# Seven block products for eight: from the MLPs' first half, 256 columns moving, to their second half, 512 columns moving

## The chip, the cores and the metric

The kernel runs on one core of one Trainium2 chip. The metric is the device time of one execution in microseconds; the kernel before takes 1494.91 us, the median of three runs (1493.44 to 1496.66).

## What is computed

A decoder trunk of two layers on 512 tokens with 1024 features. Each layer has a token mixer (a Mamba-2 SSD in layer 0, an HGRN2 in layer 1), a norm, a squared-ReLU MLP with 4096 hidden features, a second norm, and a gated embedding. The change touches the MLPs:

```python
def sq_relu_mlp(h, w1, w2):
    a = jax.nn.relu(h @ w1)
    return (a * a) @ w2

h = layer_norm(DEEPNORM_ALPHA * x + mix, ln_g[i, 0], ln_b[i, 0])
h = layer_norm(DEEPNORM_ALPHA * h + sq_relu_mlp(h, mlp_w1[i], mlp_w2[i]), ln_g[i, 1], ln_b[i, 1])
x = h + jax.nn.sigmoid(h @ ple_w_gate[i]) * (p[i] @ ple_w_proj[i])
```

## The kernel before

Every large product is made of three matmuls on fp32r operands (`mm3`, L109 to L112): each operand is split into a high part (a cast on ScalarE, ACT) and a low part (a subtraction on VectorE, DVE), and high x high, high x low and low x high are summed in PSUM. Weights come in units of 128 x 1024 floats, 512 KB: `unit` (L98) loads one through SP's queue and splits it; the split parts live in two pools, `whi` and `wlo`, of five slots each, so a sixth unit is split only when TensorE (PE) is through with the first. Splits stand some 100 places early in the program (`LEAD`). The operand named first after the arrow in a profile row is the one that moves, the second is the stationary one.

`mlp_and_gate` (L345) has two halves, cut into eight parts e of four hidden tiles each:

- `hidden(e)` makes hidden features, 128 at a time, transposed: the weights are stationary, and the 512 tokens of h.T move. A plain tile is 8 x 3 matmuls with 512 columns moving (`project`, L127). The first four tiles (e = 0) are made by halves of the tokens, 256 columns at a time, while the last tokens' norm is still under way. The result goes through ReLU and square on ACT and is split.
- `out_project(e)` multiplies the four tiles with four row tiles of `w2`: tokens are stationary, 512 columns of weights move. For each of four token chunks and two column halves it takes 12 matmuls, and DVE adds the bank to `acc` (L223): 96 matmuls and eight adds for each e.

Of the 16 pairs of hidden tiles, the first three are plain. The other 13 use Winograd's form of Strassen's product (`strassen`, L309): seven products of blocks instead of eight, with half of the tokens as a block. So each matmul moves 256 columns, and a pair costs 7 x 4 x 3 = 84 of them instead of 48 with 512. Its sums cost DVE work: sums of h.T's blocks once per layer (`block_sums`, from an unsplit copy of h.T that the norm's `keep` makes), four 512-wide sums of weights for each pair and 3.5 units to split instead of two (`weight_sums`), and seven 256-wide sums of the products out of PSUM (L329 to L343), with one copy on ACT.

The order of the work is set by the table `ORDER`: h0 b0 h1 o0 h2 o1 ... h7 o6 o7, with o7 done token chunk by token chunk, each followed by the second norm and its transposes. Engines run their instructions in the order of the program, as a scheduler with the leads has laid it out; pools decide when a tile can be written again. Four PSUM banks `pj` serve the products, two `py` the mixers and the gate. SBUF is full: the pool `b8` has nine slots of 8 KB a partition, four of which hold h.T in its two parts. GpSimd (POOL) does nothing but a few memsets at the start.

Of the kernel before, what the change touches and what calls it, by code (L numbers as in the profile page):

```python
# [9 lines left out]
F32R = mybir.dt.float32r  # L10
# [32 lines left out]
def trunk(ctx: ExitStack, tc, a):  # L43
# [24 lines left out]
    def f32(t):  # L68
        return t.bitcast(F32)

    two = dict(xs=2, sz=2, cv=2, cm=2, cbm=2)
    bufs = dict(ssd=dict(two, ss=2), mlp0=dict(z=2, S=3), hgrn=dict(two, xs=4, sz=4, cv=4, y=2, pv=2, btok=2), mlp1=dict(z=2, S=3))
# [24 lines left out]
    # ---------------------------------------------------------------- weights  # L97
    def unit(src, lead=LEAD):  # L98
        n = src.shape[1]
        with tc.high_priority(offset=lead):  # L100
            raw = mk(raws, [P, 1024], "raw")
            nc.sync.dma_start(raw[:, :n], src)
            hi = mk(whip, [P, 1024], "whi", F32R)
            nc.scalar.copy(hi[:, :n], raw[:, :n])  # L104
            lo = mk(wlop, [P, 1024], "wlo", F32R)
            nc.vector.tensor_sub(lo[:, :n], raw[:, :n], f32(hi[:, :n]))  # L106
        return hi, lo

    def mm3(out, sh, sl, mh, ml, start, stop):  # L109
        nc.tensor.matmul(out, sh, mh, start=start, stop=False)  # L110
        nc.tensor.matmul(out, sh, ml, start=False, stop=False)  # L111
        nc.tensor.matmul(out, sl, mh, start=False, stop=stop)  # L112

    class Split:
        """[128, n, 512] as high and low parts, in slots of four rows each."""
# [11 lines left out]
    def project(src, xs, ps, m=P, tok=slice(0, T)):  # L127
        """ps[m, tok] = W[:, tile].T @ x.T for a weight unit of eight row tiles."""
# [5 lines left out]
    # ---------------------------------------------------------------- constants  # L134
# [35 lines left out]
    # ---------------------------------------------------------------- layer norm and friends  # L170
# [7 lines left out]
    def layer_norm(c, gb):  # L178
        """acc[:, c] = LN(acc[:, c])"""
# [13 lines left out]
    def transpose_split(src, dst, c, keep=None):  # L193
        """dst[:, k, chunk c] = src[tokens, k-th 128 features].T, split; unsplit in keep"""
        sl = slice(c * P, (c + 1) * P)
        for q in range(2):
# [8 lines left out]
            if keep is not None:  # L205
                nc.scalar.copy(keep[q][:, :, sl], v)
# [18 lines left out]
    def out_project(w, xs, first, after=None, scale=None):  # L225
        """w: the four units of four row tiles, by halves of the columns; after(c): what follows the last of chunk c"""
# [12 lines left out]
    def norm(i):  # L239
        """the norm's result, transposed and split, and what makes its chunk c"""  # L240
        gb = ln_params(i)
        h_s = Split(8)
        keep = [mk(b8, [P, 4, T], "b8") for _ in range(2)] if i % 2 == 0 else None

        def chunk(c):
            layer_norm(c, gb)
            transpose_split(acc[:, c, :], h_s, c, keep)

        return h_s, chunk, keep
# [3 lines left out]
    def block_sums(h_s, ht):  # L253
        """the four plain and four summed blocks of h.T, as (high, low) of a row tile k"""
        b = [[ht[k][:, :, 256 * t : 256 * t + 256] for k in range(2)] for t in range(2)]

        def plain(t, k):
            sl = slice(256 * t, 256 * t + 256)
            return lambda i: (h_s.h(4 * k + i, sl), h_s.l(4 * k + i, sl))

        def summed(f, t):
            nc.scalar.copy(t[:, 0], f)
            nc.vector.tensor_sub(t[:, 1], f, f32(t[:, 0]))
            return lambda i: (t[:, 0, i, :], t[:, 1, i, :])

        sums, prev = [], None
        for i in range(4):
            f = mk(w4, [P, 4, 256], "ab"[i % 2])
            if i == 0:
                nc.vector.tensor_add(f, b[1][0], b[1][1])  # L270
            elif i == 1:
                nc.vector.tensor_sub(f, prev, b[0][0])
                s2 = f
            elif i == 2:
                nc.vector.tensor_sub(f, b[0][0], b[1][0])
            else:
                nc.vector.tensor_sub(f, b[0][1], s2)
            prev = f
            t = tmp("S", [P, 2, 4, 256], F32R) if i < 3 else mk(b8, [P, 2, 4, 256], "b8", F32R)
            sums.append(summed(f, t))  # L280
        return [plain(0, 0), plain(0, 1), plain(1, 1)] + sums

    def weight_sums(src1, src2):
        """the seven blocks of two weight units: B11, B21, B22, T1, T2, T3, B21 - T2, as (high, low, column)"""
        h = 512
        with tc.high_priority(offset=LEAD):
            r1, r2 = mk(raws, [P, 1024], "raw"), mk(raws, [P, 1024], "raw")
            nc.sync.dma_start(r1, src1)
            nc.sync.dma_start(r2, src2)

            def split(f, n=1024):
                hi = mk(whip, [P, 1024], "whi", F32R)
                nc.scalar.copy(hi[:, :n], f)  # L293
                lo = mk(wlop, [P, 1024], "wlo", F32R)
                nc.vector.tensor_sub(lo[:, :n], f, f32(hi[:, :n]))  # L295
                return hi, lo

            w1 = split(r1)
            t1, t3 = mk(w4, [P, 1024], "a"), mk(w4, [P, 1024], "b")
            nc.vector.tensor_sub(t1[:, :h], r2[:, :h], r1[:, :h])  # L300
            nc.vector.tensor_sub(t1[:, h:], r2[:, h:], t1[:, :h])
            w2 = split(t1)
            nc.vector.tensor_sub(t3[:, :h], r2[:, h:], r2[:, :h])
            nc.vector.tensor_sub(t3[:, h:], r1[:, h:], t1[:, h:])
            w3 = split(t3)
            w4_ = split(r2[:, h:], h)
        return (*w1, 0), (*w1, h), (*w4_, 0), (*w2, 0), (*w2, h), (*w3, 0), (*w3, h)

    def strassen(blocks, src1, src2, z):  # L309
        """z[:, m] = W[:, tile m].T @ h.T for two weight units"""  # L310
        a11, a12, a22, s1, s2, s3, s4 = blocks
        b11, b21, b22, t1, t2, t3, t4 = weight_sums(src1, src2)

        def product(ps, x, w):
            hi, lo, c0 = w
            for k in range(4):
                c = slice(c0 + k * P, c0 + k * P + P)
                mm3(ps, hi[:, c], lo[:, c], *x(k), k == 0, k == 3)

        def pair():  # L320
            return bank(psj, "pj")[:, :256], bank(psj, "pj")[:, :256]

        z11, z12, z21, z22 = z[:, 0, :256], z[:, 1, :256], z[:, 0, 256:], z[:, 1, 256:]
        x1, u2, u3, u5 = (tmp(tag, [P, 256]) for tag in ("x1", "u2", "u3", "u5"))
        p1, p6 = pair()
        product(p1, a11, b11)
        nc.scalar.copy(x1, p1)
        product(p6, s2, t2)
        nc.vector.tensor_add(u2, p6, x1)  # L329
        p7, p5 = pair()  # L330
        product(p7, s3, t3)
        nc.vector.tensor_add(u3, p7, u2)
        product(p5, s1, t1)
        nc.vector.tensor_add(u5, p5, u2)
        nc.vector.tensor_add(z22, p7, u5)
        p2, p3 = pair()
        product(p2, a12, b21)
        nc.vector.tensor_add(z11, p2, x1)
        product(p3, s4, b22)
        nc.vector.tensor_add(z12, p3, u5)  # L340
        p4 = bank(psj, "pj")[:, :256]
        product(p4, a22, t4)
        nc.vector.tensor_add(z21, p4, u3)  # L343

    def mlp_and_gate(layer, h_s, ht, last):  # L345
        """acc holds the normed h. Returns the next x, transposed and split, with x in acc."""
        w1, w2 = a[f"w1_{layer}"], a[f"w2_{layer}"]

        def hidden(e):
            s = Split(4)  # L350
# [693 lines left out]
```

## Time and profile before

| | before |
|---|---|
| median of three runs | 1494.91 us |
| span of the profiled execution | 1492.3 us |
| PE busy | 1479.3 us, 8848 matmuls |
| weight loads on PE (PEld) | 1280.9 us |
| DVE busy | 1096.4 us |
| ACT busy | 711.2 us |
| POOL busy | 0.9 us |
| HBM traffic | 150.07 MB, 101 GB/s mean |

The span runs from the first to the last instruction of one profiled execution; the timed runs hold 2.6 us more. Busy times of matmuls are modelled and overlap their neighbours, so what a stream of matmuls costs is read from start to start. PEld overlaps PE. A group's line gives the source line, engine, operation, tiles and shapes, the count, then busy us and mean ns, then the idle time before the group and what ended it.

### The profile page before, as it was taken

How to read it: one execution, taken by the hardware profiler on the slowest of the kernel's cores; microseconds unless marked ns; L12 is line 12 of the kernel's file. 1: busy time of each engine (PE TensorE's matmuls, PEld its weight loads, DVE VectorE, ACT ScalarE, POOL GpSimd, SP SyncE). 2: the span in 40 equal slices, each digit the busy share in tenths (PEclk: the TensorE clock that was granted, in tenths of full speed). 3: DMA queues.
4: the chain of work that ended last, by engine and by line, in shares of the span. 5: the costliest groups of instructions: out<-in, count | busy, mean ns of one | idle time of the engine just before them, and what ended most of it. 6: DMA issues, size and time to landing. Idle time of an engine off the chain costs nothing.

```text
span 1492.3 us, 21964 instructions
## 1 busy us (share of the span) xinstructions
PE 1479.3 (99%) x8848; PEld 1280.9 (86%) x8848; DVE 1096.4 (73%) x1786; ACT 711.2 (48%) x968; POOL 0.9 (0%) x8
## 2 busy tenths in 40 slices
PE   8999999999999999999999999999999999999998
PEld 5888888888989999888778998989898999998887
DVE  6998677797886777776844767769787777777673
ACT  5777455563564434444334453543364444444342
POOL 0000000000000000000000000000000000000000
PEclk9999999999999999999999999999999999999999
DMA  6433223332233323244223222222123333324322
GB/s 237 169 102 111 98 100 113 100 113 85 71 99 99 113 82 103 88 139 129 94 71 114 86 66 77 70 72 72 57 72 99 114 113 100 110 79 150 115 71 71
DMA packets 41621, 150.07 MB, mean 101 GB/s; under 512 B 4624, under 2 KB 5136, under 8 KB 41392
## 3 DMA queue, kind: packets, MB, share of 16 engines
q1 hardware_dynamic: 41520, 148.67, 30.1%
q8 instruction: 70, 1.15, 0.3%
q14 instruction: 31, 0.25, 0.1%
HBM read 146.49 MB, written 2.16 MB: 100 GB/s over the span
## 4 chain that ended last, share of the span: by engine, by line
PE 97%; DMA 1%; DVE 1%; ACT 1%; issue 0%; SPq 0%; ACTq 0%; DVEq 0%
PE pj L110 29%; PE pj L111 28%; PE pj L112 28%; PE py L782 1%; PE py L591 1%; PE pt L200 1%; PE pm L561 1%; PE py L596 1%; PE py L792 1%; PE py L827 1%; DMA raw<-in_wg 1%; DVE wlo L106 0%; PE pt L549 0%; PE py L880 0%; PE py L112 0%; PE py L110 0%
## 5 line engine op out<-in xcount | busy, mean ns | idle before, releaser
L110 PE MATMUL pj<-whi,b 128*128 128x512 f32 (+1 forms) x1096 | 401.5, 367 | 0.5 <-ACT z L414 0.5
L111 PE MATMUL pj<-wlo,b 128*128 128x512 f32 (+1 forms) x1096 | 399.3, 364 | 0.5 <-DVE wlo L106 0.5
L112 PE MATMUL pj<-whi,b 128*128 128x512 f32 (+1 forms) x1096 | 399.8, 365 | 0.0
L110 PE MATMUL pj<-b,whi 128*128 128x256 f32 (+1 forms) x1024 | 348.0, 340 | 2.1 <-ACT whi L104 2.1
L112 PE MATMUL pj<-b,wlo 128*128 128x256 f32 (+1 forms) x1024 | 344.2, 336 | 0.0
L111 PE MATMUL pj<-b,whi 128*128 128x256 f32 (+1 forms) x1024 | 343.7, 336 | 0.0
L104 ACT CAST whi<-raw 128x1024 fp32r<-128x1024 f32 x192 | 201.4, 1050 | 229.6 <-PE pj L111 133.4
L106 DVE TENSOR_TENSOR wlo<-raw,whi 128x1024 fp32r<-128x1024 f32 x192 | 233.9, 1220 | 64.4 <-ACT whi L104 62.4
L111 PEld LDWEIGHTS pj<-wlo,b 128*128 128x128 f32 x1096 | 206.8, 189 | 32.2 <-DVE wlo L106 1.0
L110 PEld LDWEIGHTS pj<-whi,b 128*128 128x128 f32 x1096 | 206.6, 189 | 32.3 <-ACT z L414 0.7
L112 PEld LDWEIGHTS pj<-whi,b 128*128 128x128 f32 x1096 | 206.7, 189 | 31.7 <-issue 0.2
L110 PEld LDWEIGHTS pj<-b,whi 128*128 128x128 f32 x1024 | 194.5, 190 | 22.0 <-ACT whi L104 4.7
L112 PEld LDWEIGHTS pj<-b,wlo 128*128 128x128 f32 x1024 | 194.4, 190 | 20.3 <-DVE b L150 1.7
L111 PEld LDWEIGHTS pj<-b,whi 128*128 128x128 f32 x1024 | 194.6, 190 | 18.3 <-issue 1.9
L293 ACT CAST whi<-raw 128x1024 fp32r<-128x1024 f32 (+1 forms) x52 | 43.4, 835 | 136.2 <-PE pj L112 110.4
L223 DVE TENSOR_TENSOR acc<-pj,acc 128x512 f32<-128x512 f32 x120 | 81.6, 686 | 35.0 <-PE pj L112 34.5
L110 PE MATMUL pj<-S,whi 128*128 128x256 f32 x312 | 87.4, 280 | 0.0
L111 PE MATMUL pj<-S,whi 128*128 128x256 f32 x312 | 87.0, 279 | 0.0
L112 PE MATMUL pj<-S,wlo 128*128 128x256 f32 x312 | 87.0, 279 | 0.0
L295 DVE TENSOR_TENSOR wlo<-raw,whi 128x1024 fp32r<-128x1024 f32 (+1 forms) x52 | 49.7, 957 | 35.0 <-ACT whi L293 35.0
L293 ACT CAST whi<-a 128x1024 fp32r<-128x1024 f32 x26 | 27.3, 1050 | 94.8 <-PE pj L111 45.5
L110 PEld LDWEIGHTS pj<-S,whi 128*128 128x128 f32 x312 | 58.7, 188 | 0.0
(217 smaller groups left out, 1810.6 us busy)
## 6 DMA issues: line engine op xcount, KB each, us to landing
raw<-in_w SPq DMA_DIRECT2D x128, 512.0 KB, 3.4
raw<-in_wssd SPq DMA_DIRECT2D x40, 512.0 KB, 3.4
a<-csd SPq DMA_DIRECT2D x16, 512.0 KB, 4.0
raw<-in_wso SPq DMA_DIRECT2D x16, 512.0 KB, 3.3
raw<-in_wg SPq DMA_DIRECT2D x16, 512.0 KB, 3.8
raw<-in_whvg SPq DMA_DIRECT2D x16, 512.0 KB, 3.3
raw<-in_whq SPq DMA_DIRECT2D x16, 512.0 KB, 3.3
raw<-in_who SPq DMA_DIRECT2D x8, 512.0 KB, 3.3
```

The source lines that it names most:

```text
L104: nc.scalar.copy(hi[:, :n], raw[:, :n])
L106: nc.vector.tensor_sub(lo[:, :n], raw[:, :n], f32(hi[:, :n]))
L110: nc.tensor.matmul(out, sh, mh, start=start, stop=False)
L111: nc.tensor.matmul(out, sh, ml, start=False, stop=False)
L112: nc.tensor.matmul(out, sl, mh, start=False, stop=stop)
L200: nc.tensor.transpose(pt[:, j * P : (j + 1) * P], src[:, k * P : (k + 1) * P], ident)
L223: nc.vector.tensor_add(d, ps, d)
L293: nc.scalar.copy(hi[:, :n], f)
L295: nc.vector.tensor_sub(lo[:, :n], f, f32(hi[:, :n]))
L561: nc.tensor.matmul(pst_[:, c * P : (c + 1) * P], btok[:, c, :], xw[:, c].rearrange("p h q -> p (h q)"), start=True, stop=True)
L591: nc.tensor.matmul(yd[64 * r : 64 * r + 64, sl], xdt[:, 2 * c + r, :], m[:, r, sl], start=True, stop=True)
L596: nc.tensor.matmul(yo[:, c * P : (c + 1) * P], pv[:, c - 1].rearrange("p h q -> p (h q)"), cm[:, c * P : (c + 1) * P], start=True, stop=True,)
```

## The change

The first half becomes plain throughout: all hidden tiles are 24 matmuls with 512 columns moving. The second half takes Strassen's form, in four groups g of 1024 hidden features (8 tiles). A product of blocks has 256 tokens x 512 hidden features, stationary, and 512 x 512 weights, moving: two token chunks, four row tiles, three matmuls each, 24 matmuls with 512 columns. Seven of them make a group: 168 matmuls instead of 192.

- The seven sums of the result are not formed by DVE. Products that share a term go into the same PSUM banks, one after another ("chains"): x takes a11, s2, s1, s4 in turn (banks `py`), y takes s3 and a22 (`pj`), z takes a12 alone. After each product DVE adds the bank as it stands to the block of `acc` that needs it (L314, L316), and PE goes on adding to the bank: 14 adds of 128 x 512 for each group. PE's next write to a bank waits for DVE's read.
- `block_product` loads a group's eight units of `w2` into ten slots `r` of their own and makes T1 to T4 from them with eight sums of 128 x 1024 on GpSimd (L290, L292, L321, L325), in place where it can. The two first pairs stand 220 places early (`SUMS`).
- `hidden(g, p)` makes four tiles; `half_blocks` (L257) turns them into their half of the group's seven blocks: four sums of 128 x 2 x 256 on GpSimd, in place and each dependent on the one before (L269 to L275), and for each block a cast on ACT (L263) and a subtraction on DVE (L264). Five blocks live in `b8`, s3 and s4 in a pool of two.
- `ORDER` is h00 h01 h10 o0 h11 h20 o1 h21 h30 h31 o2 o3. In o3 the products come as a11, a12, s2, s1, s4, then the norm of the first two token chunks, then s3, a22 and the norm of the others.
- `block_sums`, `weight_sums`, `strassen` and the unsplit copy of h.T go away; a scratch area for DMA descriptors is set to 1024 bytes.

```diff
-PLAIN = 3
-ORDER = [(w[0], int(w[1])) for w in "h0 b0 h1 o0 h2 o1 h3 o2 h4 o3 h5 o4 h6 o5 h7 o6 o7".split()]
+ORDER = "h00 h01 h10 o0 h11 h20 o1 h21 h30 h31 o2 o3".split()
+SUMS = 220
...
+    def half_blocks(blk, z0, z1, p):
+        ks = slice(2 * p, 2 * p + 2)
+        a11, a12, a21, a22 = z0[:, :, :256], z1[:, :, :256], z0[:, :, 256:], z1[:, :, 256:]
+        def put(name, f):
+            hi, lo = blk[name][:, 0, ks, :], blk[name][:, 1, ks, :]
+            nc.scalar.copy(hi, f)
+            nc.vector.tensor_sub(lo, f, f32(hi))
+        put("a22", a22)
+        put("a11", a11)
+        put("a12", a12)
+        nc.gpsimd.tensor_add(a22, a21, a22)
+        put("s1", a22)
+        nc.gpsimd.tensor_sub(a21, a11, a21)
+        put("s3", a21)
+        nc.gpsimd.tensor_sub(a11, a22, a11)
+        put("s2", a11)
+        nc.gpsimd.tensor_sub(a12, a12, a11)
+        put("s4", a12)
...
+    def block_product(w, blk, first, after=None):
+        with tc.high_priority(offset=SUMS):
+            raw = {}
+            for i, j in ((0, 0), (0, 1), (1, 1), (1, 0)):
+                raw[i, j] = []
+                for u in range(2):
+                    raw[i, j].append(tmp("r", [P, 1024]))
+                    nc.sync.dma_start(raw[i, j][u], w[i][j][u])
+            t1, t2, t3, t4 = raw[0, 1], [tmp("r", [P, 1024]) for _ in range(2)], raw[0, 0], raw[1, 0]
+            for u in range(2):
+                nc.gpsimd.tensor_sub(t1[u], raw[0, 1][u], raw[0, 0][u])
+            for u in range(2):
+                nc.gpsimd.tensor_sub(t2[u], raw[1, 1][u], t1[u])
...
+        def product(x, f, name, start, i, j, then=None):
+            us = [split(v) for v in f]
+            if then is not None:
+                with tc.high_priority(offset=LEAD):
+                    then()
+            if start:
+                banks[name] = [bank(psy, "py%d" % c) if name == "x" else bank(psj, "pj") for c in range(2)]
+            t = blk[x]
+            for c in range(2):
+                ps = banks[name][c]
+                sl = slice(c * P, (c + 1) * P)
+                for k in range(4):
+                    hi, lo = us[k // 2]
+                    ks = slice((k % 2) * 512, (k % 2 + 1) * 512)
+                    w_ = hi[:, ks], lo[:, ks]
+                    mm3(ps, t[:, 0, k, sl], t[:, 1, k, sl], *w_, start and k == 0, k == 3, skip_group_check=True)
+                d = acc[:, 2 * i + c, j * 512 : (j + 1) * 512]
+                if (i, j) in seen:
+                    nc.vector.tensor_add(d, ps, d)
+                else:
+                    nc.vector.scalar_tensor_tensor(d, d, ALPHA, ps, ALU.mult, ALU.add)
+            seen.add((i, j))
...
+        product("a11", raw[0, 0], "x", True, 0, 0, sums3)
+        product("a12", raw[1, 0], "z", True, 0, 0, sums4)
+        product("s2", t2, "x", False, 1, 0)
+        p7 = lambda: product("s3", t3, "y", True, 1, 1)
+        p5 = lambda: product("s1", t1, "x", False, 1, 1)
+        p4 = lambda: product("a22", t4, "y", False, 1, 0)
+        p3 = lambda: product("s4", raw[1, 1], "x", False, 0, 1)
+        if after is None:
+            for f in (p7, p5, p4, p3):
+                f()
+        else:
+            p5(), p3(), after(0), after(1)
+            p7(), p4(), after(2), after(3)
```

The first place where the order of instructions matters to what follows is DVE's queue in a second-half block of layer 0. Before, in the middle of the MLP: `a`, `b` and `raw` are the weights of a Strassen pair to come and their sums, `pj` the block's banks, `z` a hidden tile.

```order
L300 TENSOR_TENSOR a_4379<-raw_4372,raw_4371 128x512
L223 TENSOR_TENSOR acc_94<-pj_4244,acc_94 128x512
L301 TENSOR_TENSOR a_4379<-raw_4372,a_4379 128x512
L303 TENSOR_TENSOR b_4380<-raw_4372 128x512
L374 TENSOR_TENSOR b_689_3963<-z_4098,b_688_3962 128x1024
L304 TENSOR_TENSOR b_4380<-raw_4371,a_4379 128x512
L223 TENSOR_TENSOR acc_94<-pj_4258,acc_94 128x512
```

The sums of weights stand between the adds, and no other engine makes any. Now, at the start of o2: `py` and `pj` are the chains' banks, `wlo` the low parts of the product's weights, and the rows of L264 write the blocks of h30 and h31 (`a` and `b` are their hidden tiles).

```order
L264 TENSOR_TENSOR b_823_4918<-b_4988,b_823_4918 128x512
L112 TENSOR_TENSOR wlo_5322<-r_5238,whi_5320 128x1024
L314 TENSOR_TENSOR acc_94<-py_877_5254,acc_94 128x512
L264 TENSOR_TENSOR b_822_4917<-b_5138,b_822_4917 128x512
L264 TENSOR_TENSOR b_821_4916<-b_5138,b_821_4916 128x512
L314 TENSOR_TENSOR acc_94<-py_878_5255,acc_94 128x512
L112 TENSOR_TENSOR wlo_5326<-r_5239,whi_5324 128x1024
L264 TENSOR_TENSOR b_824_4919<-a_4922,b_824_4919 128x512
L112 TENSOR_TENSOR wlo_5356<-r_5222,whi_5354 128x1024
```

Both halves' blocks are written while o2 runs, between its splits and its adds. The second place is GpSimd's queue over the same stretch of the program, where before there is no row; r are the weights of group 3.

```order
L269 TENSOR_TENSOR b_4988<-a_4922,b_4988 128x2x256
L271 TENSOR_TENSOR a_4922<-a_4922 128x2x256
L273 TENSOR_TENSOR a_4922<-b_4988,a_4922 128x2x256
L275 TENSOR_TENSOR b_4988<-b_4988,a_4922 128x2x256
L269 TENSOR_TENSOR b_5138<-a_5072,b_5138 128x2x256
L271 TENSOR_TENSOR a_5072<-a_5072 128x2x256
L273 TENSOR_TENSOR a_5072<-b_5138,a_5072 128x2x256
L275 TENSOR_TENSOR b_5138<-b_5138,a_5072 128x2x256
L290 TENSOR_TENSOR r_5504<-r_5504,r_5500 128x1024
L290 TENSOR_TENSOR r_5506<-r_5506,r_5502 128x1024
```

The eight block sums come first and T1 of group 3 behind them; T2, T3 and T4 of group 3 follow in o2 and o3.

More of the change, by code (lines that the diff above doesn't have):

```diff
@@ L102, in unit, with split, mm3 @@
             nc.sync.dma_start(raw[:, :n], src)
+        return split(raw[:, :n], lead)
+    def split(f, lead=LEAD):
+        n = f.shape[1]
+        with tc.high_priority(offset=lead):
             hi = mk(whip, [P, 1024], "whi", F32R)
-            nc.scalar.copy(hi[:, :n], raw[:, :n])
+            nc.scalar.copy(hi[:, :n], f)
             lo = mk(wlop, [P, 1024], "wlo", F32R)
-            nc.vector.tensor_sub(lo[:, :n], raw[:, :n], f32(hi[:, :n]))
+            nc.vector.tensor_sub(lo[:, :n], f, f32(hi[:, :n]))
         return hi, lo
[L109 to L112, printed above, removed]
+    def mm3(out, sh, sl, mh, ml, start, stop, **kw):
+        nc.tensor.matmul(out, sh, mh, start=start, stop=False, **kw)
+        nc.tensor.matmul(out, sh, ml, start=False, stop=False, **kw)
+        nc.tensor.matmul(out, sl, mh, start=False, stop=stop, **kw)
     class Split:
@@ L283, in weight_sums @@
[L283 to L343, printed above, removed]
@@ L663, in trunk @@
         pend = cur
-    h_s, after, ht = norm(0)
+    h_s, after = norm(0)
     ssd_out(*outs.pop(0), after)
     begin("mlp0")
-    x_s = mlp_and_gate(0, h_s, ht, False)
+    x_s = mlp_and_gate(0, h_s, False)
     begin("hgrn")
@@ L922, in trunk @@
             pass
-    h_s, after, ht = norm(2)
+    h_s, after = norm(2)
     out_project(a["who"][4:8], halves[1], False, after)
     begin("mlp1")
-    mlp_and_gate(1, h_s, ht, True)
+    mlp_and_gate(1, h_s, True)
     phase[1].__exit__(None, None, None)
```

125 lines of the change are left out of this document (53 added, 72 removed).

## The prediction

> **What bounds the kernel now.** I read the page first: busy time by engine, then the chain that ended last.
>
> ```profile
> span 1492.3 us, 21964 instructions
> PE 1479.3 (99%) x8848; PEld 1280.9 (86%) x8848; DVE 1096.4 (73%) x1786; ACT 711.2 (48%) x968; POOL 0.9 (0%) x8
> PE 97%; DMA 1%; DVE 1%; ACT 1%; issue 0%; SPq 0%; ACTq 0%; DVEq 0%
> ```
>
> TensorE (PE) is busy for all but 13 us, and 97% of the chain is PE. So a change is worth what it takes from PE's stream of matmuls, less the waits that it puts into that stream. Durations in that stream overlap, so I price it by stretches from the first matmul's start to the next kind's start. The windows below are such stretches of layer 0's MLP: two blocks of the second half's plain products (96 matmuls, 512 columns moving), two pairs of Strassen's (168 matmuls, 256 columns moving), and the whole from the last plain pair to the gate.
>
> ```profile
> core 0: us, PE busy (x) PEld busy (x) DVE busy (x) ACT busy (x) POOL busy (x), PEclk, DMA share, GB/s
> 559.20:580.98 21.78, 21.78 (x98) 18.02 (x97) 15.66 (x22) 6.86 (x7) 0.00 (x0) 1.00 0.26 87
> 539.19:559.20 20.01, 20.01 (x170) 20.01 (x169) 14.89 (x24) 11.56 (x13) 0.00 (x0) 1.00 0.37 117
> ...
> 412.91:742.50 329.59, 329.06 (x1980) 293.99 (x1979) 244.82 (x344) 145.73 (x163) 0.00 (x0) 1.00 0.33 106
> ```
>
> (Counts include a neighbour or two cut by the edge.) A 512-column matmul costs 21.78/96 = 0.2269 us, a 256-column one 20.01/168 = 0.1191, so two of the latter cost 5% more than one of the former. In the Strassen stretch the weight loads (PEld) are busy for all 20.01 us, in the plain one for 18.02 of 21.78: with 256 columns moving, a load is barely hidden. The clock is 1.00 in all. In the whole stretch DVE is busy for 74% and PE waits 0.5 us, so DVE, ACT and DMA have room now. That room is what the list of waits shows: ACT stands waiting for PE to release a split slot.
>
> ```profile
> ACT whi L293 <- PE pj L112: 159.2, 47, 8.5
> ACT whi L104 <- PE pj L111: 133.4, 89, 8.8
> ```
>
> **The change part by part.** *PE.* In each layer 13 of 16 pairs of hidden tiles lose Strassen's form: 13 x 84 matmuls of 256 columns become 26 x 24 of 512. By the windows that is 6.5 x 20.01 = 130.1 us against 6.5 x 21.78 = 141.6, so +11.5. The second half loses one of its eight blocks' worth, 768 matmuls to 672: -21.78. Net -10.3 a layer, **-20.6 us** in all. The counts in the order of instructions bear it out: 512-column matmuls rise by 1056, 256-column ones fall by 2184, and 1056 x 0.2269 - 2184 x 0.1191 = -20.5. The by-form groups hold those 2184: three lines of 312, and three of 544 less 384 in the first tiles, which stay.
>
> ```profile
> L110 PE MATMUL pj<-S,whi 128*128 128x256 f32 x312 | 87.4, 280 | 0.0
> L110 PE MATMUL pj<-b,whi 128*128 128x256 f32 x544 | 153.7, 283 | 0.0
> ```
>
> *DVE.* The groups that price its share, with one of ACT's, and then three neighbours on DVE's timeline:
>
> ```profile
> L106 DVE TENSOR_TENSOR wlo<-raw,whi 128x1024 fp32r<-128x1024 f32 x192 | 233.9, 1220 | 64.4 <-ACT whi L104 62.4
> L223 DVE TENSOR_TENSOR acc<-pj,acc 128x512 f32<-128x512 f32 x120 | 81.6, 686 | 35.0 <-PE pj L112 34.5
> L295 DVE TENSOR_TENSOR wlo<-raw,whi 128x512 fp32r<-128x512 f32 x26 | 17.9, 689 | 15.9 <-ACT whi L293 15.9
> L293 ACT CAST whi<-raw 128x512 fp32r<-128x512 f32 x26 | 16.1, 621 | 106.2 <-PE pj L112 101.6 <-PE pj L111 4.6
> L332 DVE TENSOR_TENSOR u<-pj,u 128x256 f32<-128x256 f32 x26 | 10.9, 421 | 11.0 <-PE pj L112 11.0
> L183 DVE BATCH_NORM_STATS2 lnst<-acc 128x6 f32<-128x512 f32 x32 | 21.3, 685 | 0.3
> L190 DVE SCALAR_TENSOR_TENSOR acc<-acc,lnmv,a 128x1024 f32<-128x1024 f32 x16 | 20.5, 1284 | 0.5
> ```
>
> ```profile
> 570.03 1.23 DVE L295 TENSOR_TENSOR wlo<-a,whi 128x1024 fp32r<-128x1024 f32 x1 [0.66 <-ACT whi L293]
> 571.17 0.68 DVE L223 TENSOR_TENSOR acc<-pj,acc 128x512 f32<-128x512 f32 x1
> 571.77 1.22 DVE L295 TENSOR_TENSOR wlo<-b,whi 128x1024 fp32r<-128x1024 f32 x1
> ```
>
> From start to start a 1024-wide split takes 1.14 us and anything 512 wide 0.60. Per layer DVE loses 52 weight sums (31.2), 91 sums of Strassen's products (at 0.42, 38.2), 19.5 splits in the first half (22.2), 16 splits of the hidden tiles (18.2), eight 1024-wide steps of the block sums (9.1) and eight adds (4.8). It gains 24 splits in the second half (27.4) and 56 low parts of the blocks (33.6). Net -62.7 us of some 245. All of it lies beside PE, so the loss is worth nothing by itself.
>
> *ACT* trades casts for casts and keeps near its 145.7 us of 329.6: no term. *DMA* moves the same 512 KB units; their median landing is 3.4 us:
>
> ```profile
> raw<-in_w SPq DMA_DIRECT2D x128, 512.0 KB, 3.4
> ```
>
> On SP's queue the eight `r` loads of a group now stand among the first half's units and wait for DVE's last splits of the group before. Behind them stands the fourth tile of the next `h`, which PE wants 3 x 5.45 = 16 us after that product's end: hidden. At the MLP's start seven of them stand ahead of h01's first unit, which is wanted 23 us later: hidden at 3.4 us each even one by one (24 us), up to 1 us. On ACT, the cast of the next group's s4 waits for the running product's last matmul, with the Relus and casts of the next tiles queued behind; four split units are ahead of it in ACT's order, 21.8 us of PE: hidden.
>
> *GpSimd* gets 32 sums of 1024 columns and 32 of 512 a layer. The trace has no such operation. Its nearest row is a memset on the same engine:
>
> ```profile
> 0.73 0.51 POOL L163 MEMSET cm<- 32x512 f32 x1 [0.29 <-POOLq L1032]
> ```
>
> One written stream of 512 columns takes 0.51 us, so a sum of 1024 costs between 1.0 (reads beside the write) and 3.1 us (two reads and a write in turn). I take 2.04, the two reads in turn, and half of that for 512: 98 us of a layer's 330. It is not the bound; at 3.1 it would be 147. (The Trainium skill's "GPSIMD Engine Reference", "Performance versus the Vector engine", measured 4497 ns for a sum of 2048 columns; from it I estimate 2.25 for 1024, unconfirmed by any row here.) The chain of four dependent sums after each `h`, each with a cast and a subtraction behind it, is some 4 x (1.02 + 0.6 + 0.6) = 9 us long; a group's blocks are wanted one `h` (21.8 us) later, so it is covered.
>
> *Where PE can wait.* In a product PE spends 24 x 0.2269 = 5.45 us, and DVE owes it two splits and two adds, 3.5 us, and about one low part, 0.6. Five split slots let splits run at most 1.5 products ahead. A bank in the chain is written again one product later, in o3 already after 12 matmuls (2.7 us); there DVE's add (0.60) with one split ahead of it (1.14) just fits. In o0 and o1 DVE has 14 splits, 14 adds, 7 low parts: 28.6 of 38.1 us. The tight place is o2 with o3, 76.2 us of PE back to back, because the blocks of h30 and h31 can only be written once the old h.T is released, at o2's start. By the order DVE has 29 splits, 14 low parts, 28 adds, 6 statistics, 4 norm steps and 4 transposed low parts there: 33.1 + 8.4 + 16.8 + 3.6 + 5.1 + 2.4 = 69.4 us. GpSimd has eight sums of each width: 24.5 us. If the two engines run beside each other without effect, 69.4 fits and I allow 1 us a layer for handovers in the fixed order. If a DVE instruction with two SBUF operands and a GpSimd sum take turns, then 46.6/76.2 = 61% of GpSimd's 24.5 us falls on DVE as delay, 15 us: 84.4, 8.2 too much. No row shows which. The 1.5 products that the slots run ahead (8.2 us at best, and partly used) absorb some; I take half, **4 us a layer, +8**. In o0 and o1 turns would cost 53% of up to 16 us, giving 37.1 of 38.1: nothing.
>
> (By the Trainium skill's "SBUF — State Buffer", "Who interferes with whom", the turns are real: a DVE instruction with two SBUF inputs and a GpSimd instruction that reads SBUF exclude each other, the later one blocked to the end. With the estimate of 2.25 us the excess would be 9.7 us, and half of it twice makes 1484.0. No row here can show it.)
>
> *Sum.* The profiled span is 1492.3, and the median of the runs 1494.9, 2.6 above it, which lies around the span and stays. 1494.9 - 20.6 + 8 = **1482.3 us**.
>
> **The rivals.** *No interference.* GpSimd costs DVE nothing; only handovers remain: 1494.9 - 20.6 + 2 = 1476.3. For it: DVE's total falls, and PE waited 0.5 us in 330 at 74% DVE. Against: 91% in o2 and o3.
>
> *Strict turns, nothing absorbed.* 8.2 us a layer: 1494.9 - 20.6 + 16.4 = 1490.7. This is the page's lock without the slots' help. Against it: slots filled before o2 begins are work that DVE has already done.
>
> *GpSimd slow and in strict turns: slower than before.* At 3.1 us, o2 with o3 has 37.2 us of GpSimd, 22.7 of delay, 15.9 too much; o0 and o1 have 24.8 each, 13.1 of delay, 41.7 of 38.1, 3.6 too much. That is 23.1 a layer: 1494.9 - 20.6 + 46.2 = 1520.5, or 1497.4 with half absorbed. It decides from 10.3 us of waits a layer on. Against it: it needs the dearest price of GpSimd and the hardest contention together.
>
> That the matmuls are not saved can be ruled out by the order, and their prices stand in this trace.
>
> **How the numbers follow.** Forecast (1478 to 1488): 0.44. No interference (1474 to 1478): 0.27. Strict turns (1488 to 1494): 0.17. Slower: 0.12. The range that leaves out the slow case and the top of the strict one is **1474 to 1494**. About 0.2% (3.0 us) is what a measurement can tell from no change: faster is below 1491.9, slower above 1497.9. Faster takes the first two cases and two thirds of the third, 0.82; within 0.2% is the rest of the third and a quarter of the fourth, 0.09; slower 0.09.
>
> **What would show it.** Right: 512-column matmuls at 0.227 us in both halves; 13 pairs' worth of first half in 141.6 us; PE's waits in o2 and o3 some 4 us a layer, released by DVE's low parts or adds; DVE's splits longer than 1.22 us where GpSimd runs. Splits at 1.22 throughout and no PE wait there show the first rival; waits of 8 us and above there, or GpSimd sums near 3 us with waits in o0 and o1 too, the others. The prediction is wrong at its root if PE waits elsewhere, as at the start of an MLP, or if the 512-column price moves.

## The result and the profile after

The changed kernel takes **1511.64 us** (median of 4 runs, 1508.68 to 1514.75) where the kernel before, run beside it, takes 1495.79 (1493.44 to 1497.12). The ratio is 1.0107, 95% interval 1.0092 to 1.0122: slower by about 16 us, where 1482.3 was forecast. The profiled run itself took 1508.68, its span is 1506.9, so 1.8 us lie around it.

The page first: totals by engine, and the chain's shares.

```profile
span 1506.9 us, 19584 instructions
PE 1470.1 (98%) x7720; PEld 1222.1 (81%) x7720; DVE 1101.0 (73%) x1544; ACT 723.5 (48%) x1020; POOL 274.8 (18%) x136
PE 88%; DVE 9%; DMA 2%; ACT 1%; issue 0%; POOL 0%; SPq 0%; ACTq 0%; DVEq 0%
```

PE has 1128 matmuls fewer, as forecast, but is busy only 9 us less and idle for 37 us instead of 13. DVE, which lost 242 instructions, is as busy as before, and holds 9% of the chain where it held 1%. To see where the time went I cut both MLPs from their first matmul to the same later mark (in layer 0 the gate's 96 matmuls with 512 columns, in layer 1 the last matmul with output `py`). First the kernel before, then the changed one.

```profile
412.91:799.07 386.16, 384.68 (x2262) 339.60 (x2261) 274.97 (x381) 167.09 (x191) 0.00 (x0) 1.00 0.32 104
1113.35:1481.38 368.03, 368.03 (x2158) 326.52 (x2157) 261.40 (x364) 156.91 (x177) 0.00 (x0) 1.00 0.31 102
```

```profile
core 0: us, PE busy (x) PEld busy (x) DVE busy (x) ACT busy (x) POOL busy (x), PEclk, DMA share, GB/s
413.49:806.00 392.51, 380.87 (x1699) 311.11 (x1697) 280.52 (x265) 179.91 (x227) 124.89 (x60) 0.98 0.28 91
1121.86:1495.87 374.01, 362.94 (x1593) 296.48 (x1592) 266.83 (x248) 169.69 (x213) 124.96 (x60) 0.99 0.27 88
```

The MLPs grew by 6.35 and 5.98 us where 10.3 less each was worked out from the matmuls alone, so some 16.5 us a layer came on top, of which the forecast allowed 4. Part of it is idle time (392.51 - 380.87 = 11.6 us in layer 0, against 1.5 before), part a lower clock: 0.98 over the whole stretch. The rest of the span's 14.6 us lies outside (1.6 from the gate to layer 1's MLP, 0.6 ahead of the first MLP). Now stretch by stretch in layer 0: a W1 stretch, o1, o2, the wait between o2 and o3, and the start of o3.

```profile
495.46:539.01 43.55, 43.55 (x194) 36.04 (x193) 24.76 (x21) 20.70 (x28) 15.55 (x8) 1.00 0.26 87
539.01:577.43 38.42, 38.42 (x169) 31.55 (x168) 33.99 (x30) 18.32 (x21) 18.82 (x9) 1.00 0.37 122
642.74:684.79 42.05, 40.27 (x169) 32.36 (x167) 41.85 (x34) 20.71 (x25) 25.33 (x13) 0.96 0.37 125
684.79:690.42 5.63, 0.16 (x1) 0.00 (x0) 5.63 (x4) 2.08 (x3) 3.40 (x2) 0.70 0.00 0
691.24:694.00 2.76, 2.76 (x7) 2.19 (x8) 2.76 (x2) 0.00 (x0) 1.69 (x1) 0.50 0.02 6
```

W1's 192 matmuls take 0.2268 each and o1's 168 take 38.42, 0.3 over 168 x 0.2269. In o2 DVE is busy for 41.85 of 42.05 us; then PE waits for 6.3 us, and starts o3 at half its clock. The first matmul of o3 on PE's timeline, and two rows of the list of waits, name the releaser:

```profile
691.24 0.77 PE L116 MATMUL py<-whi,b 128*128 128x512 f32 x1 [6.29 <-DVE acc L314]
PE py L116 <- DVE acc L314: 15.5, 5, 6.3
PE pj L117 <- DVE wlo L112: 4.4, 4, 1.8
```

Five waits for DVE's adds, of which two of 6.3 us, and four for its splits. What DVE and GpSimd did there stands on their timelines, DVE's first:

```profile
676.01 0.68 DVE L314 TENSOR_TENSOR acc<-py,acc 128x512 f32<-128x512 f32 x1
676.61 3.08 DVE L112 TENSOR_TENSOR wlo<-r,whi 128x1024 fp32r<-128x1024 f32 x1
679.62 0.68 DVE L314 TENSOR_TENSOR acc<-py,acc 128x512 f32<-128x512 f32 x1
680.22 3.10 DVE L112 TENSOR_TENSOR wlo<-r,whi 128x1024 fp32r<-128x1024 f32 x1
683.24 0.68 DVE L314 TENSOR_TENSOR acc<-pj,acc 128x512 f32<-128x512 f32 x1
683.84 3.09 DVE L112 TENSOR_TENSOR wlo<-r,whi 128x1024 fp32r<-128x1024 f32 x1
686.85 0.68 DVE L314 TENSOR_TENSOR acc<-pj,acc 128x512 f32<-128x512 f32 x1
687.45 3.04 DVE L112 TENSOR_TENSOR wlo<-r,whi 128x1024 fp32r<-128x1024 f32 x1
690.42 0.68 DVE L314 TENSOR_TENSOR acc<-py,acc 128x512 f32<-128x512 f32 x1
```

```profile
676.22 2.39 POOL L292 TENSOR_TENSOR r<-r,r 128x1024 f32<-128x1024 f32 x1 [7.62 <-DVE wlo L112]
679.83 2.41 POOL L292 TENSOR_TENSOR r<-r,r 128x1024 f32<-128x1024 f32 x1 [1.22 <-issue]
683.46 2.39 POOL L321 TENSOR_TENSOR r<-r,r 128x1024 f32<-128x1024 f32 x1 [1.23 <-DVE wlo L112]
687.07 2.34 POOL L321 TENSOR_TENSOR r<-r,r 128x1024 f32<-128x1024 f32 x1 [1.23 <-DVE wlo L112]
```

The two engines alternate. A sum starts at 676.22, during DVE's add from PSUM, and the split that DVE issues at 676.61 lasts 3.08 us, not 1.22: it stays until 1.1 us after the sum's end at 678.61. The next sum starts 0.14 us after the split's end at 679.69, and so on, six times in a row (the last group's T2, T3 and T4; the first four are shown). The adds, with one operand in PSUM, take 0.68 throughout. A split and an add now take 3.61 us from start to start, a product needs two of each, 7.2 us, and PE takes 5.45 for it.

### The profile page after: what moved, and what is told of

It is laid out like the page before. It is cut to its first block, busy times and chain, and to the rows that moved or that the text cites. A ratio compares the mean times of both kernels' runs of the same rounds, so it can differ in the third digit from the quotient of the medians.

```text
span 1506.9 us, 19584 instructions
## 1 busy us (share of the span) xinstructions
PE 1470.1 (98%) x7720; PEld 1222.1 (81%) x7720; DVE 1101.0 (73%) x1544; ACT 723.5 (48%) x1020; POOL 274.8 (18%) x136
## 4 chain that ended last, share of the span: by engine, by line
PE 88%; DVE 9%; DMA 2%; ACT 1%; issue 0%; POOL 0%; SPq 0%; ACTq 0%; DVEq 0%
PE pj L116 23%; PE pj L117 23%; PE pj L118 23%; DVE wlo L112 4%; PE py L116 3%; PE py L118 3%; PE py L117 3%; DVE b L264 2%; PE py L778 1%; PE py L587 1%; DVE acc L314 1%; PE pm L557 1%; PE pt L206 1%; PE py L592 1%; DMA a<-in_pT 1%; DVE blk L264 1%
## 5 line engine op out<-in xcount | busy, mean ns | idle before, releaser
L116 PE MATMUL pj<-b,whi 128*128 128x512 f32 (+1 forms) x1024 | 392.0, 383 | 1.2 <-ACT whi L110 1.2
L118 PE MATMUL pj<-b,wlo 128*128 128x512 f32 (+1 forms) x1024 | 388.1, 379 | 0.0
L117 PE MATMUL pj<-b,whi 128*128 128x512 f32 (+1 forms) x1024 | 387.5, 379 | 0.0
L112 DVE TENSOR_TENSOR wlo<-r,whi 128x1024 fp32r<-128x1024 f32 x112 | 194.0, 1737 | 89.7 <-ACT whi L110 89.7
L116 PE MATMUL pj<-whi,b 128*128 128x512 f32 (+1 forms) x712 | 252.3, 355 | 0.5 <-ACT sg L410 0.5
L117 PE MATMUL pj<-wlo,b 128*128 128x512 f32 (+1 forms) x712 | 249.6, 351 | 0.8 <-DVE wlo L112 0.8
L118 PE MATMUL pj<-whi,b 128*128 128x512 f32 (+1 forms) x712 | 250.1, 351 | 0.0
L110 ACT CAST whi<-r 128x1024 fp32r<-128x1024 f32 x112 | 116.8, 1048 | 189.6 <-PE pj L117 60.9
L290 POOL TENSOR_TENSOR r<-r,r 128x1024 f32<-128x1024 f32 x16 | 45.1, 2826 | 767.6 <-DMA r<-in_w 760.0
L116 PEld LDWEIGHTS pj<-whi,b 128*128 128x128 f32 x712 | 134.7, 189 | 17.7 <-ACT sg L410 0.7
L118 PEld LDWEIGHTS pj<-whi,b 128*128 128x128 f32 x712 | 134.5, 189 | 17.0 <-issue 0.2
L116 PE MATMUL py<-whi,b 128*128 128x512 f32 x192 | 77.2, 402 | 15.5 <-DVE acc L314 15.5
L118 PE MATMUL py<-whi,b 128*128 128x512 f32 x224 | 88.8, 398 | 0.0
L264 DVE TENSOR_TENSOR b<-b,b 128x512 fp32r<-128x512 f32 x48 | 62.7, 1322 | 21.5 <-ACT b L263 21.3
L117 PE MATMUL py<-wlo,b 128*128 128x512 f32 x192 | 76.6, 399 | 0.6 <-DVE wlo L112 0.6
L321 POOL TENSOR_TENSOR r<-r,r 128x1024 f32<-128x1024 f32 x16 | 39.8, 2485 | 125.0 <-DVE wlo L112 125.0
```

The lines of the kernel that those rows point to most:

```text
L116: nc.tensor.matmul(out, sh, mh, start=start, stop=False, **kw)
L117: nc.tensor.matmul(out, sh, ml, start=False, stop=False, **kw)
L118: nc.tensor.matmul(out, sl, mh, start=False, stop=stop, **kw)
L264: nc.vector.tensor_sub(lo, f, f32(hi))
L290: nc.gpsimd.tensor_sub(t1[u], raw[0, 1][u], raw[0, 0][u])
L321: nc.gpsimd.tensor_sub(t3[u], t2[u], raw[0, 0][u])
```

## The theories and the experiments

**Theory A**: a GpSimd sum and a DVE instruction with two SBUF operands take strict turns; where the last group's sums fall beside o2 and o3, which stand back to back on PE, DVE falls behind and PE waits, and loses clock after the wait. **Rivals**: B, DVE has too much work there with or without GpSimd; C, the latency of GpSimd's dependent sums is on the path, not the turns; D, the fixed order alone is at fault.

**Who makes the sums.** Three kernels put sums on DVE: all (lines L269 to L325), the weight sums alone, the block sums alone.

```diff
-        nc.gpsimd.tensor_add(a22, a21, a22)
+        nc.vector.tensor_add(a22, a21, a22)
...
-                nc.gpsimd.tensor_sub(t1[u], raw[0, 1][u], raw[0, 0][u])
+                nc.vector.tensor_sub(t1[u], raw[0, 1][u], raw[0, 0][u])
```

> All 128 block sums and weight sums issue on DVE instead of GpSimd. Theory A (a GpSimd sum and a DVE instruction with two SBUF operands take strict turns, so that a 1024-wide sum costs DVE's queue 2.4 us; bunched in o2 and o3): on DVE itself a sum costs 1.14 us start to start at 1024 columns and 0.60 at 512, so o2 with o3 holds 69.4 + 8 x 1.74 = 83.3 us of DVE instead of some 97. Splits go back to 1.22 us everywhere, PE's wait between o2 and o3 falls below 2 us, its clock stays at 1.00, and the time is 1483 to 1491, I say 1486. Rival B (DVE simply has too much work there, and GpSimd costs it nothing): 13.9 us more of DVE in each layer's tight place, so 1525 or more. Rival C (the latency of GpSimd's dependent sums, without turns): a gain that comes from the block sums alone, 1490 to 1500.

Measured: 1488.95 us (1487.63 to 1490.16), ratio to before 0.9960, 95% 0.9945 to 0.9975. B falls: with 128 more instructions DVE is faster. The page of this kernel, its by-form groups, and then the same groups in the changed kernel:

```profile
PE 1466.0 (98%) x7720; PEld 1218.4 (82%) x7720; DVE 1087.0 (73%) x1672; ACT 723.7 (49%) x1020; POOL 0.9 (0%) x8
```

```profile
L112 DVE TENSOR_TENSOR wlo<-r,whi 128x1024 fp32r<-128x1024 f32 x112 | 136.2, 1222 | 80.4 <-ACT whi L110 79.4
L264 DVE TENSOR_TENSOR b<-b,b 128x512 fp32r<-128x512 f32 x48 | 32.2, 688 | 4.1 <-ACT b L263 4.1
L325 DVE TENSOR_TENSOR r<-r,r 128x1024 f32<-128x1024 f32 x16 | 19.6, 1223 | 0.4
```

```profile
L112 DVE TENSOR_TENSOR wlo<-r,whi 128x1024 fp32r<-128x1024 f32 x112 | 194.0, 1737 | 89.7 <-ACT whi L110 89.7
L264 DVE TENSOR_TENSOR b<-b,b 128x512 fp32r<-128x512 f32 x48 | 62.7, 1322 | 21.5 <-ACT b L263 21.3
L325 POOL TENSOR_TENSOR r<-r,r 128x1024 f32<-128x1024 f32 x16 | 42.5, 2665 | 23.9 <-DVE wlo L112 23.9
```

Splits of `r` fall from a mean of 1737 ns to 1222, low parts from 1322 to 688. DVE's busy time with all the sums is 1087.0 us, without them 1101.0: **what GpSimd took off DVE it gave back as delay**.

> Only the 64 weight sums (1024 columns) issue on DVE; the block sums stay on GpSimd. Theory A: in o2 and o3 eight turns of 2.4 us become eight DVE instructions of 1.14, 10 us less a layer; the wait of 6.6 us between o2 and o3 and the half clock behind it (3.8 us) go, the wait at s3 (2.8 to 3.7 us) stays: 1491, between 1486 and 1496. Rival B (overload without turns): 9 us of DVE more a layer, 1525 to 1530. Rival C (latency of the block sums' chain): 1509 to 1513.

Measured: 1493.46 (1491.72 to 1496.10), ratio 0.9990, 0.9981 to 1.0000.

> Only the 64 block sums (512 columns) issue on DVE; the weight sums stay on GpSimd. Theory A: the six weight sums in a row at the end of o2 are still there and still take turns with the splits, so the wait of 6.6 us between o2 and o3 stays; the wait at s3 shrinks to 1 to 2 us: 1505, between 1500 and 1509. Rival B (overload without turns): 4.8 us of DVE more a layer, about 1521. Rival C (latency of the block sums' chain): 1490 to 1500.

Measured: 1502.47 (1501.08 to 1508.28), ratio 1.0059, 1.0039 to 1.0079. Both fall on A's side: of the 22.7 us that all sums gain, the weight sums alone bring 18.2, the block sums alone 9.2. C had it the other way round. In the profile of the kernel with only the block sums on DVE, the wait between o2 and o3 is still there, at 3.5 us where I expected 6.6 (the profiled run took 1508.28 us, the longest of its five).

**Reads or latency.** Each sum becomes two fills of the same tile, in the same place of GpSimd's order.

```diff
-                nc.gpsimd.tensor_sub(t2[u], raw[1, 1][u], t1[u])
+                nc.gpsimd.memset(t2[u], 0.5)
+                nc.gpsimd.memset(t2[u], 0.5)
```

> In the changed kernel's own order each GpSimd sum becomes two fills of the same tile with a constant: GpSimd's instructions keep their places and about their time (2 x 1.0 us for 1024 columns, where a sum that DVE does not hold up took 2.4), but read nothing from SBUF. It leaves the seven-product sums out: the products multiply constants. Theory A (turns between GpSimd's reads and DVE's two-operand reads): the splits go back to 1.22 us everywhere, the wait between o2 and o3 and the half clock behind it go: 1481, between 1476 and 1487. Rival C (the latency of GpSimd's instructions, or their writes alone): the waits in o2 and o3 stay, 1500 to 1512.

Measured: 1478.98 us (1477.30 to 1480.43), ratio 0.9894, 0.9879 to 0.9909. The groups and the two MLP stretches, cut at the same marks as above:

```profile
L112 DVE TENSOR_TENSOR wlo<-r,whi 128x1024 fp32r<-128x1024 f32 x112 | 136.5, 1222 | 156.9 <-ACT whi L110 156.9
L333 POOL MEMSET r<- 128x1024 f32 x16 | 15.3, 958 | 0.6
```

```profile
414.87:793.31 378.44, 375.87 (x1698) 308.40 (x1697) 220.63 (x265) 178.99 (x226) 83.84 (x118) 1.00 0.29 94
1107.51:1467.67 360.16, 359.75 (x1594) 295.29 (x1593) 207.01 (x248) 168.76 (x212) 83.91 (x118) 1.00 0.28 91
```

GpSimd holds its places for 2 x 0.96 us instead of 2.4, and DVE's splits are at 1222 ns: writes do not delay them, reads do. PE's list of waits has none for an add. The fills are a fifth shorter than the sums, so this kernel alone would not rule out C; with the two before it, it does. The Trainium skill says just this in "SBUF — State Buffer", "Who interferes with whom" (a DVE instruction with two SBUF inputs contends with a GpSimd instruction that reads SBUF, not with one that only writes; whoever is later is blocked to the end), and here the runs agree. The MLPs are 7.7 and 7.9 us shorter than before, of the 10.3 worked out. PE's matmuls in layer 0 take 375.87 us here and 380.87 in the changed kernel, so 5.0 of the 14.1 us between the two lie in the same matmuls running slower, which is clock, and 9.1 are waits.

**The place.** If the turns hurt only beside o2 and o3, a quarter of the sums should hold nearly all of the loss. Two kernels: the last group's sums on DVE, and the complement.

```diff
-            half_blocks(blocks[g], *zs, p)
+            half_blocks(blocks[g], *zs, p, nc.vector if g == 3 else nc.gpsimd)
...
-                block_product(w, blocks.pop(g), g == 0, after if g == 3 else None)
+                block_product(w, blocks.pop(g), g == 0, after if g == 3 else None, nc.vector if g == 3 else nc.gpsimd)
```

Both functions take the engine of their sums as their last argument; the complement has `g < 3` in place of `g == 3`.

> In the changed kernel's own order, only the sums of the last group (8 weight sums and 8 block sums a layer, a quarter of all) issue on DVE; the other three quarters stay on GpSimd and go on taking turns. Theory A with its place (turns cost only where o2 and o3 stand back to back with the last group's sums beside them): nearly all that moving every sum gained, 1488 to 1493, I say 1490. If a turn costs about the same wherever it falls: a quarter of that gain, 1511.6 - 22.7/4 = 1506.

Measured: 1493.31 (1491.82 to 1494.38), ratio 0.9985, 0.9975 to 0.9995; 0.3 above A's range.

> The complement: the sums of the first three groups (three quarters) issue on DVE, the last group's stay on GpSimd. Theory A with its place: hardly any gain, 1507 to 1512, I say 1510, with the wait between o2 and o3 and the half clock behind it still there. If a turn costs about the same wherever it falls: three quarters of the gain, 1511.6 - 17.0 = 1494.6.

Measured: 1509.83 (1509.28 to 1512.04), ratio 1.0095, 1.0080 to 1.0110. The last group's quarter of the sums holds 18.3 of the 22.7 us; taking the turns out everywhere else gains 1.8. PE's waits for adds, of the kernel with the last group on DVE and of the complement:

```profile
PE py L116 <- DVE acc L314: 7.4, 8, 1.7
```

```profile
PE py L116 <- DVE acc L314: 17.6, 6, 6.3
```

**The order.** h31 moves between o2 and o3, with all sums on GpSimd.

```diff
-ORDER = "h00 h01 h10 o0 h11 h20 o1 h21 h30 h31 o2 o3".split()
+ORDER = "h00 h01 h10 o0 h11 h20 o1 h21 h30 o2 h31 o3".split()
```

> The sums stay on GpSimd; h31 moves from before o2 to between o2 and o3, so that o2 and o3 no longer stand back to back on PE. Theory A: the turns stay (splits of 3.1 us beside weight sums), but the weight sums of group 3 now fall beside h31's Strassen products, where DVE has slack: the wait of 6.6 us and the half clock behind it go; the blocks of h31 are wanted at once by o3, which bares some 4 us of their chain: 1500, between 1494 and 1506. Rival D (only the order is at fault, the turns cost nothing): the waits in o2 and before o3 go altogether, 1480 to 1487. Under rival B (overload) about 1485 to 1490, with splits of 1.22 us.

Measured: **1486.84 us** (1485.88 to 1488.61), ratio 0.9948, 0.9933 to 0.9963. This is better than A's 1494 to 1506, and the turns are still there, by the group of the splits; then PE's waits for adds:

```profile
L112 DVE TENSOR_TENSOR wlo<-r,whi 128x1024 fp32r<-128x1024 f32 x112 | 182.6, 1636 | 90.0 <-ACT whi L110 90.0
```

```profile
PE py L116 <- DVE acc L314: 2.1, 2, 1.0
```

The stretch of layer 0's MLP, cut as above:

```profile
413.29:794.04 380.75, 376.95 (x1698) 308.20 (x1697) 275.95 (x265) 180.28 (x227) 126.66 (x60) 1.00 0.29 93
```

DVE is busy for 275.95 us of layer 0's MLP, against 220.63 with fills: 55 us more, and the stretch is only 2.3 us longer. So D is half right: the turns cost DVE time wherever they fall, and PE time only where DVE has none to spare. (D expected 1480 to 1487 with turns that cost nothing; DVE pays for them here too.) On GpSimd's timeline the last group's T3 and T4 now stand beside h31's plain products (on PE from 659.21 to 681.00; I had called them Strassen's). Three of their four sums:

```profile
668.66 2.40 POOL L321 TENSOR_TENSOR r<-r,r 128x1024 f32<-128x1024 f32 x1 [1.22 <-DVE wlo L112]
672.48 2.39 POOL L325 TENSOR_TENSOR r<-r,r 128x1024 f32<-128x1024 f32 x1 [1.43 <-DVE wlo L112]
677.92 2.39 POOL L325 TENSOR_TENSOR r<-r,r 128x1024 f32<-128x1024 f32 x1 [3.04 <-DVE wlo L112]
```

**A better kernel.** The new order was joined with sums on DVE (the edits above), then with a new order of o3's products and a new order of the blocks.

> h31 between o2 and o3, and all sums on DVE. In the run with the new order alone PE still waited 2.6 us a layer for DVE at s1 and s4 of o3, behind low parts of 1.8 and a split of 2.3 us that took turns. Theory A: these turns go: 2 to 4 us less than that run, 1483 to 1485. Rival B (DVE's load decides now): the sums add 1.7 us of DVE per pair beside the blocks of h31, 1487 to 1492.

Measured: 1486.45 (1486.14 to 1486.68), ratio 0.9945, 0.9928 to 0.9961. The same as with the sums on GpSimd, and above my 1483 to 1485: with the place mended, the turns that are left make no difference in time that these runs can tell.

> h31 between o2 and o3, the weight sums on DVE, the block sums on GpSimd. Theory A: turns remain only with the block sums, which stand beside the first half, where PE takes 43.5 us from weights that need one split of 1.22 us per 5.45: 1484 to 1486, within 1 us of the kernel with all sums on DVE, and not slower than the one with all on GpSimd. Rival B: half of the slowdown that it expects there, 1487 to 1490.

Measured: 1487.53 (1486.39 to 1488.43), ratio 0.9951, 0.9936 to 0.9966. Within 1.1 us of both, and 1.5 above where I had set its upper end.

```diff
-            p5(), p3(), after(0), after(1)
-            p7(), p4(), after(2), after(3)
+            p5(), p7(), p3(), after(0), after(1)
+            p4(), after(2), after(3)
```

> h31 between o2 and o3, sums on GpSimd, and in o3 the product s3 (its own banks) moves between s1 and s4, which follow each other in the same two banks: DVE then has 5.4 us instead of 2.7 to add a bank before PE wants it again. The 2.6 us of waits and slow matmuls at s4 go, 5.3 over both layers, but the first two rows of norm 2 start one product later, with one product of PE behind them instead of two. Theory A (handover of a bank): 1482 if that product still covers the norm, 1488 if it doesn't; I say 1484. If the wait is the split's (weights not ready) and not the bank's, no gain: 1487 or more.

Measured: 1492.43 (1491.70 to 1493.51), ratio 0.9983, 0.9974 to 0.9993: 5.6 us worse than the new order alone. I had put the wait in the wrong place. Its profile keeps both waits in full:

```profile
PE py L116 <- DVE acc L314: 2.1, 2, 1.1
PE pt L206 <- DVE b L210: 1.8, 2, 0.9
PE py L118 <- DVE b L264: 1.0, 2, 0.5
```

The waits for the add and for the low part `b` of L264 stand between s2 and s1 and in s2, ahead of the moved product. The edit left the norm with one product behind it instead of two, and three waits a layer for the copies and low parts of the norm's transposes (0.9 us for `pt`, and two of 0.4) are new. They are the larger part of the 2.6 us by which layer 0's stretch from s2 to the gate is longer here than with the new order alone; the rest is not shown.

```diff
-        put("s3", a21)
         nc.gpsimd.tensor_sub(a11, a22, a11)
         put("s2", a11)
         nc.gpsimd.tensor_sub(a12, a12, a11)
         put("s4", a12)
+        put("s3", a21)
```

> h31 between o2 and o3, sums on GpSimd, and in each pair of tiles the blocks s2 and s4 are cast and split before s3, which is wanted last in o3. In the run with the new order alone PE waited in o3 for the low part of s2 (0.5 us, with slow matmuls behind it) and then for the add of s2's second bank (1.0), 2.6 us a layer. If it is the low part that comes late: 1482 to 1484. If it is only the add behind a split in its turn: 1486 to 1488, no gain.

Measured: 1488.10 us (1486.91 to 1488.66), ratio 0.9946, 0.9931 to 0.9961. No gain: the wait for the low part is gone from the list, but those for the adds rise from 2.1 us in two to 3.8 in four.

> The same with all sums on DVE. Its run without this edit waited 0.9 us a layer for an add in o3. If the low part of s2 comes late there too: 1483 to 1485; if not, 1486 to 1487. Theory A has no turns here, so it expects this kernel within 1.5 us of the one with the sums on GpSimd.

Measured: **1486.21** (1485.43 to 1486.54), ratio 0.9933, 0.9919 to 0.9948, the fastest of the kernels that compute all the sums, level with the new order and all sums on DVE. The kernels with the new order, all but the one with o3 rearranged, beat both of the two that were compared, by about 0.5% and 1.6%; the one-word change of the order is enough for it.

## Why the prediction was wrong

- **PE's saving: right in the main.** 512-column matmuls cost 0.2268 us in W1 and 0.2287 in o1 where PE does not wait, the counts are as said, and without the turns and the sums 15.6 of the 20.6 us show in the two MLPs (7.7 and 7.9). Of the 2.5 us a layer that are missing, PE's idle time holds 1.1 in layer 0 and 0.4 in layer 1 (2.57 and 0.41 with fills, 1.48 and none before), as "1 us a layer for handovers" had it. The other 1.5 and 2.0 us are in the matmuls' own time; o1's 0.3 us are of this kind, and no run here says why.
- **The waits at the start of an MLP, in the first half, in o0 and o1: right.** None; o1 lost 0.3 us.
- **DVE's own work: nearly right in size.** It was to fall by 62.7 us a layer; with fills its busy time fell from 274.97 to 220.63, 54 us, in layer 0. With GpSimd's reads beside it, it rose to 280.52.
- **GpSimd's price: right within its bounds.** An undisturbed sum of 1024 columns takes 2.39 us, taken at 2.04. (The estimate of 2.25 from the Trainium skill's "GPSIMD Engine Reference", "Performance versus the Vector engine", is 6% low.) The means of 2.5 to 2.8 us in the groups hold turns that GpSimd lost.
- **The step that failed: "I take half, 4 us a layer".** The turns were named and the place was right, o2 with o3; but 84.4 us of DVE were set against 76.2 of PE as if they were spread over the whole stretch, and slots that run ahead were to absorb half. The trace of after has 14.2 us there in layer 0, 3.7 in s3 of o2 and 10.5 from o2's end into o3, slow clock included. The turns come in a burst: each of the six sums starts as one split ends, T2's two after o2's last two splits, T3's and T4's, which are made in place, after o3's first four. PE's first matmul of o3 waits for the add at 690.42. From the add at 676.01 to that one DVE runs four pairs of add and split with turns, 14.4 us; four pairs without turns take 4 x 1.74 = 7.0. Without the turns that add would have started at 683.0, before PE was through with o2 (684.79); with them PE waits 6.3 us. Counted from the MLP's start, three of the four splits in between are for o3: the slots that run ahead absorbed nothing here, since DVE's fixed order put their splits in front of the add. The kernels with the last group's sums on DVE and with h31 moved show it: the first removes a quarter of the turns and 18.3 us, the second leaves the turns and removes 24.8.
- **In the burst a turn costs more than the overlap rule gave it.** I let 61% of GpSimd's time fall on DVE. In the burst each sum lengthens a split by 3.08 - 1.22 = 1.86 us, 78% of its 2.39, since each engine starts as soon as the other is done. Issued on DVE it would have cost 1.14. Over the whole of layer 0's MLP the delay, against the kernel with fills, is 280.52 - 220.63 = 59.9 us for 124.89 of GpSimd, 48%: the rule was not too low for the average, but for the burst.
- **A term that was missing: the clock.** It was read as 1.00 in all stretches of before and held there. In layer 0's MLP it cost 5.0 us, part of the 14.2.
- **The case that came true.** The time fell into the fourth one's span (1497.4 to 1520.5), which had 0.12, and past its point of 10.3 us of waits a layer. Its mechanism was not the one: GpSimd was at 2.4, not 3.1 us, and o0 and o1 lost nothing. What I called "strict turns, nothing absorbed" happened, at 1.7 times the price that an average over the stretch gave it (14.2 for 8.2). That the chance of a slower kernel was so small came from the same average.

**Open**: between the gate and the next MLP the profiles differ by up to 2.2 us from one kernel to the next, in code that none of them edits; no run here tells where that comes from. Of the 20.6 us, the kernels with the new order give 7.4 to 9.3, all but the one with o3 rearranged; the 2.6 us a layer at s2 and s1 of o3 are known by place, but putting s2 first gained nothing.

## What to carry to other kernels

Work moved to GpSimd isn't off DVE if it reads SBUF while DVE's instructions have two operands there: price it as a delay of DVE, in a burst by most of the sum's length (here 1.86 of 2.39 us), and compare that with what DVE would have needed itself (1.14). Check a queue's capacity where its work bunches, product by product against its deadline, not as an average over the stage; the bunch sits where two engines release each other in turn (here a split a sum, with the next split right behind it). Work that runs ahead helps only if nothing urgent stands behind it in the same queue. Before moving work between engines, try moving the stage with slack next to the one without: one word of the order gave as much as the best change of engine (24.8 and 22.7 us).

## What was not expected of the hardware

A short wait can cost PE its clock. After a wait of 1.78 us in s3 of o2 (a split was late), PE ran on at full speed for half a microsecond and then for 3.4 us at half. In layer 1 of the same run a wait of 1.77 us stands at the same place, and nothing slow follows it. The clock of the slow stretch stands below them:

```profile
662.63 0.50 PE L117 MATMUL pj<-wlo,blk 128*128 128x512 f32 x1 [1.78 <-DVE wlo L112]
...
663.21 0.62 PE L116 MATMUL pj<-whi,blk 128*128 128x512 f32 x1
663.63 0.63 PE L117 MATMUL pj<-wlo,blk 128*128 128x512 f32 x1
...
1371.01 0.50 PE L117 MATMUL pj<-wlo,blk 128*128 128x512 f32 x1 [1.77 <-DVE wlo L112]
1371.34 0.40 PE L118 MATMUL pj<-whi,blk 128*128 128x512 f32 x1
1371.58 0.40 PE L116 MATMUL pj<-whi,blk 128*128 128x512 f32 x1
```

```profile
663.00:666.40 3.40, 3.40 (x10) 2.68 (x9) 3.40 (x2) 0.00 (x0) 2.01 (x2) 0.53 0.46 154
```

Matmuls start every 0.43 us in the slow stretch instead of 0.23: eight of them lose 1.6 us, behind a wait of 1.78. In the kernel with only the block sums on DVE, the waits of 3.48 and of 1.99 us at o3's start were each followed by 3.5 us of it; in the kernel with only the last group's sums on GpSimd, a wait of 2.15 us in layer 0 was not, and one of 2.01 in layer 1 was. Of the thirteen waits of 1.5 to 2.2 us in o2 and o3 of the profiles here, four have such a stretch behind them; the waits of 1.0 us in the run with the new order have none. So the length of the wait alone does not decide it. The Trainium skill, "TensorE: Matmul & The Clock Gate", "What's actually happening", has the half clock come after an idle window of some 3.4 us in a grid that runs freely: the length of the slow stretch agrees with it, but a wait of little more than half such a window was enough here. That the place of a wait in the grid decides is not shown by any run. A stall of PE of 2 us can thus cost nearly 4.
